# The first MLP matrices in token layout, with seven block products for eight on half of the rows

## The chip, the cores and the metric

One NeuronCore of a Trainium2 chip runs the whole program; the other seven are idle. The metric is the device time of one execution in microseconds (us), the median of several runs.

## The reference, cut to what matters

A two-layer decoder trunk on 256 positions of width 2048, all in float32: a recurrent mixer (layer 0) or dilated attention (layer 1), an output projection with residual, then an MLP with residual. The change is in the MLP:

```python
D_MODEL, SEQ, DEPTH = 2048, 256, 2
D_FF = 4 * D_MODEL
def squared_relu_mlp(h, w1, w2):
    return jnp.square(jax.nn.relu(h @ w1)) @ w2
...
h = h + squared_relu_mlp(rms_norm(h, norm_mlp[layer]), mlp_w1[layer], mlp_w2[layer])
```

The two MLPs hold 2 x 2 x 2048 x 8192 weights, about 62% of all weight bytes that the kernel reads.

## The kernel before, in words

**Precision.** Every large product is made from three: each operand x is split into hi (a rounded copy) and lo = x - hi, and hi*hi, hi*lo and lo*hi are added up in PSUM. `Weights.split` (L102 to L106) does this for weights: ScalarE (ACT) copies hi (L105), VectorE (DVE) subtracts to lo (L106).

**Units.** All weights come as units of 128 x 2048 floats, 1 MB each. `units` is the list of them in the order of use; `unit()` (L166) hands out the next one and calls `fetch()` (L111) so that the loads run about two units ahead. Loads go out on the queue of SyncE (SP). `hi`, `lo` and `raw` have three buffers each. `hi` of a unit can be written when TensorE (PE) has finished the unit three places before it.

**Each MLP runs in four quarters** of 2048 hidden features (`mlp`, L685). A quarter has two stages.

- *First matrix (w1).* 16 units, each for 128 hidden features. `project` (L354) with `cross` (L206) holds the weights still and streams the activations: for each of 16 blocks of the input one matmul of 512 columns (weight hi against activation hi and lo side by side) and one of 256 (weight lo against activation hi). The result has features on partitions, so `folded` (L225), the squared relu (L691) and `split_to` (L233) write it straight into `bufb`, the input of the second matrix. `sums` (L623) prepares four combinations of blocks in `forms`.
- *Second matrix (w2).* Here activations are held still and 512 weight columns stream (`products`, L633). On half of the rows the 2 x 2 block product is done with seven products instead of eight: the weight blocks a, t1, t2, c, t3, d, t4 of `PRODUCTS` (L883) are sums of units, made by `combine` (L127) in place: `a` += t1, `a` += t2, `a` += d on DVE (L143) and t1 += the unit of t2 by an accumulating DMA from the queue of GpSimd (POOL, L139). The units "n" are plain rows. One such unit is 12 matmuls, a plain one 24 (two halves j of the tokens). A quarter has two such pairs (n0 = 0 and n0 = 2) of 11 units. `to_x` (L654) adds the banks into the residual `xall`. The tiles `a` and `t1` have one buffer each, so the next pair's `a` can be loaded only when the last split that reads `a` is done.

**Order.** A list scheduler orders each engine's instructions at build time; on the chip ACT and DVE run theirs strictly in that order. Matmuls of the large products and the transposes through PE (`turn`, L179) are chained by hand in program order (`chain`, L174). Work in `later` is run by `flush()` (L184). `urgent` raises the priority of what empties PSUM, `stream` that of loads and splits.

**Transposes before.** `to_features` (L598) turns the residual back to features on partitions for the next stage, 8 transposes of 128 x 128 a time, only after the output projections and after the MLP of layer 0.

Of the kernel before, what the change touches and what calls it, by code (L numbers as in the profile page):

```python
# [20 lines left out]
P = 128  # L21
# [20 lines left out]
def trunk_kernel(ctx, tc, x, xtok, cols, tab, masks, pos, fin, w_in, w_gate, w_out, w_qkv, w_o, w1, w2, out):  # L42
# [28 lines left out]
    def plan2(i, products):  # L71
        if not products:
            units.extend((w2, i + u) for u in range(8))
            return
        for what, u in PRODUCTS:
            units.append((w2, None if u is None else i + u, what))
# [34 lines left out]
    def fetch():  # L111
        u = at[0]
        if u >= len(units):
            return
        at[0] += 1
        src, i = units[u][:2]
        with stream():
            if len(units[u]) > 2:
                combine(u, src, i, units[u][2])
# [3 lines left out]
            made[u] = Weights(r, 2048 if src is w2 or src is w1 and i % 64 > 2 else 1024)  # L123
# [3 lines left out]
    def combine(u, src, i, what):  # L127
# [10 lines left out]
        if T3_DMA and what == "t2":  # L138
            nc.gpsimd.dma_start(held["t1"], src[i], accum_op=OP.add)  # L139
        if T3_DMA and what == "t3":  # L140
            add = None
# [83 lines left out]
    def folded(p, name="z", bufs=None, home=None):  # L225
        with urgent():
            t = tmp.tile([P, S], F32, name="t1", bufs=2)
            A.copy(t, p[:, S:])  # L228
            z = (home or tmp).tile([P, S], F32, name=name, bufs=bufs)
            V.tensor_tensor(z, p[:, :S], t, OP.add)  # L230
        return z

    def split_to(dst, src, gain=None):  # L233
        if gain is None:
            A.copy(dst[:, :S], src)  # L235
            V.tensor_tensor(dst[:, S:], src, dst[:, :S].bitcast(F32), OP.subtract)
# [26 lines left out]
    class FirstNorm:  # L263
# [3 lines left out]
        def add(self, blk):  # L267
            self.n += 1
            q = tmp.tile([P, S], F32, name="t1", bufs=2)
            A.activation(q, blk, AF.Square)  # L270
            if self.n == 1:
                self.ss.append(tmp.tile([P, S], F32, name="q", bufs=1))
# [94 lines left out]

    nrm = FirstNorm()
# [47 lines left out]
    def scaled(p, z, acc=None):  # L416
        with urgent():
            if acc is direct:
                V.tensor_tensor(z, p[:, :S], rs, OP.mult)
            else:  # L420
                t = tmp.tile([P, S], F32, name="t1", bufs=2)
# [9 lines left out]
    vgs = mixers.enter_context(tc.tile_pool(name="vgs", bufs=1))  # L431
    wk = mixers.enter_context(tc.tile_pool(name="wk", bufs=2))
# [131 lines left out]
    def lru_out(b):  # L564
# [3 lines left out]
        q = tmp.tile([P, S], F32, name="q", bufs=1)  # L568
# [17 lines left out]
    rot = mixers.enter_context(tc.tile_pool(name="rot", bufs=1))  # L586
# [11 lines left out]
    def to_features(n, gname):  # L598
        def work():
            with urgent():  # L600
                for half in range(2):
                    p = psc.tile([P, 2, S], F32, name="pl", bufs=2)
                    for j in range(2):
                        for i in range(2):
                            k = 4 * n + 2 * half + i
                            turn(p[:, i, j * P:j * P + P], xres[:, j, k * P:k * P + P])
                    for i in range(2):
                        k = 4 * n + 2 * half + i
                        split_to(bufa[:, k], p[:, i], col(gname, k))
        later.append(work)  # L610

    def out_project(src, gname, kgs):
        nrm = Norm()
        for n in range(4):
            add_res(tokens(src, 4 * n, bufb, kgs), n, nrm)
            to_features(n, gname)
# [4 lines left out]
    spot = []  # L621

    def sums(k, z1, z2):  # L623
        t = pair.tile([P, 512], F32, name="sums")
        a11, a21, a12, a22 = z1[:, :P], z1[:, P:], z2[:, :P], z2[:, P:]
        V.tensor_tensor(t[:, :P], a21, a22, OP.subtract)
        V.tensor_tensor(t[:, P:2 * P], t[:, :P], a11, OP.subtract)
        V.tensor_tensor(t[:, 2 * P:3 * P], a11, a21, OP.subtract)
        V.tensor_tensor(t[:, 3 * P:], a12, t[:, P:2 * P], OP.add)
        A.copy(forms[:, k, 0], t)  # L630
        V.tensor_tensor(forms[:, k, 1], t, forms[:, k, 0].bitcast(F32), OP.subtract)

    def products(i0, n0, nrm, r2, r2n, done):  # L633
        n1 = n0 + 1
        i0 += 4 * n0
        plain = lambda j, k: (bufb[:, k, j * P:j * P + P], bufb[:, k, S + j * P:S + j * P + P])
        form = lambda f, k: (forms[:, k, 0, f * P:f * P + P], forms[:, k, 1, f * P:f * P + P])
        side = {"a": lambda i: plain(0, 2 * i), "d": lambda i: plain(0, 2 * i + 1), "t4": lambda i: plain(1, 2 * i + 1),
                "t1": lambda i: form(0, i), "t2": lambda i: form(1, i), "t3": lambda i: form(2, i),
                "c": lambda i: form(3, i)}  # L640
        alpha, delta, gamma = (pmm.tile([P, 512], F32, name="p") for _ in range(3))
        beta = psc.tile([P, 512], F32, name="po" if n0 else "pd", bufs=1)
        opened = []
# [10 lines left out]
        def to_x(bank, j, n, sign=1, last=False):  # L654
            at = slice(n * 512, n * 512 + 512)
            with urgent():
                V.scalar_tensor_tensor(xres[:, j, at], bank, (r2 if sign > 0 else r2n)[:, j:j + 1], xres[:, j, at],  # L657
                                       op0=OP.mult, op1=OP.add)
                if nrm and last:
                    nrm.add(j, n)  # L660

        after_product = {"a": [(beta, 0, n0, 1)], "t1": [(alpha, 1, n1, 1)], "t2": [(beta, 0, n1, -1)],
                         "t3": [(beta, 1, n1, -1, True)]}
        bank = {"a": beta, "t1": alpha, "t2": beta, "c": alpha, "t3": beta, "d": gamma, "t4": beta}
        for what, u in PRODUCTS:
            w = unit(w2, None if u is None else i0 + u)
            if what != "n":
                times(bank[what], w, side[what])
                for job in after_product.get(what, ()):
                    to_x(*job)  # L670
                if what == "t3":
                    done(n1)
                if what == "t4":
                    flush()
                continue
            n, g = divmod(u, 4)
            for j in (1, 0) if n else (0, 1):
                times({(0, 0): gamma, (0, 1): beta, (1, 0): alpha, (1, 1): delta}[n, j], w,
                      lambda i, j=j, g=g: plain(j, 4 * g + i))
                if g == 3:  # L680
                    to_x({(0, 0): gamma, (0, 1): beta, (1, 0): alpha, (1, 1): delta}[n, j], j, n + n0, 1, (n, j) != (1, 1))
            flush()
        done(n0)

    def mlp(layer, nrm, nxt, gname):  # L685
        r2 = None
        for q in range(4):
            for m in range(16):
                z = folded(project(w1, layer * 64 + q * 16 + m, bufa), "zp", 3, pair)
                with urgent():  # L690
                    V.scalar_tensor_tensor(z, z, 0.0, z, op0=OP.max, op1=OP.mult)  # L691
                    split_to(bufb[:, m], z)
                if m < 8 and m % 2:
                    sums(m // 2, zs, z)
                zs = z
                if r2 is None:
                    r2 = nrm.inv_mean()
                    r2n = tmp.tile([P, 2], F32, name="r2n", bufs=1)
                    V.tensor_scalar(r2n, r2, -1.0, None, op0=OP.mult)
                    if not gname:  # L700
                        lut(spare, epsc, AF.Sqrt)
                    spot[:] = [after(V.memset(spare, 0.0), [])]
            ends = nxt if q == 3 else None

            def done(n):
# [4 lines left out]
                elif n != LAST:  # L710
                    at = slice(n * 512, n * 512 + 512)
                    with urgent():
                        for j in range(2):
                            V.tensor_tensor(xres[:, j, at], xres[:, j, at], fing[:, at], OP.mult)

            for n in range(4):
                if n < 2 * PAIRS:
                    if n % 2 == 0:
                        products(layer * 64 + q * 16, n, ends, r2, r2n, done)
                else:  # L720
                    ps = tokens(w2, layer * 64 + q * 16 + 4 * n, bufb)
                    add_res(ps, n, ends, r2)
                    done(n)

    pairs = ExitStack()
    pair = pairs.enter_context(tc.tile_pool(name="pair0", bufs=1))
    forms = pair.tile([P, 4, 2, 512], F32R, name="forms", align_bytes=LINE)
# [4 lines left out]

    ppi = rot.tile([32, S], I32, name="ppi")
    nc.gpsimd.dma_start(ppi, bass.AP(tensor=pos.tensor, offset=pos.offset, ap=[[0, 32], [1, S]]))
    ang = rot.tile([32, S], F32, name="ang")
    cosT = rot.tile([32, S], F32, name="cosT")
    sinT = rot.tile([32, S], F32, name="sinT")
    after(V.tensor_copy(ang, ppi), spot)
    V.tensor_scalar(ang, ang, tab_[:32, TC_FREQ:TC_FREQ + 1], None, op0=OP.mult)
    MAGIC = 12582912.0  # L740
    V.tensor_scalar(cosT, ang, 1.0 / (2.0 * math.pi), None, op0=OP.mult)
    V.tensor_scalar(cosT, cosT, MAGIC, None, op0=OP.add)
    V.tensor_scalar(cosT, cosT, MAGIC, None, op0=OP.subtract)
    rest = 2.0 * math.pi
    for bits in (5, 13, 21, None):
        part = rest if bits is None else math.floor(rest * 2.0 ** bits) / 2.0 ** bits
        rest -= part
# [241 lines left out]
```

## Time and profile before

| | us |
|---|---|
| median of 3 runs | 2202.48 (2202.17 to 2202.95) |
| the profiled execution | 2203.3 |
| its span, first to last instruction | 2201.2 |
| DVE busy | 1673.1 (76%) |
| ACT busy | 1110.8 (50%) |
| weight loads of PE (PEld) busy | 1897.6 (86%) |

In rows of the profile the name left of the arrow is the tile that is written, those right of it are read; "x16" is a count; for grouped instructions "busy, mean ns" follow the bar, then the idle time of the engine before them and who ended it. A timeline row is start, length, engine, line, operation. A row of the chain of waits is start, length, what. PEclk is the share of full clock that PE was granted. 431.25 MB were moved by DMA, 196 GB/s in the mean.

### The profile page before, as it was taken

How to read it: one execution, taken by the hardware profiler on the slowest of the kernel's cores; microseconds unless marked ns; L12 is line 12 of the kernel's file. 1: busy time of each engine (PE TensorE's matmuls, PEld its weight loads, DVE VectorE, ACT ScalarE, POOL GpSimd, SP SyncE). 2: the span in 40 equal slices, each digit the busy share in tenths (PEclk: the TensorE clock that was granted, in tenths of full speed). 3: DMA queues.
4: the chain of work that ended last, by engine and by line, in shares of the span. 5: the costliest groups of instructions: out<-in, count | busy, mean ns of one | idle time of the engine just before them, and what ended most of it. 6: DMA issues, size and time to landing. Idle time of an engine off the chain costs nothing.

```text
span 2201.2 us, 29711 instructions
## 1 busy us (share of the span) xinstructions
PE 2180.7 (99%) x12004; PEld 1897.6 (86%) x12004; DVE 1673.1 (76%) x2294; ACT 1110.8 (50%) x1371; POOL 14.7 (1%) x21
## 2 busy tenths in 40 slices
PE   9999999999999999999999999999999999999998
PEld 8999998888888888888888888888888888888886
DVE  7766796578877877877867778556797687687787
ACT  7444485545444444544655445445454445445444
POOL 0000000000000000000000000000000000000000
PEclk9999999999999999999999999999999999999999
DMA  8444446555655755765655554655566567566553
GB/s 314 154 162 164 154 154 229 184 197 192 233 197 184 248 194 167 245 216 157 217 200 173 172 179 166 225 191 185 164 215 246 176 205 249 191 191 248 188 195 115
DMA packets 61081, 431.25 MB, mean 196 GB/s; under 512 B 6784, under 2 KB 7552, under 8 KB 9488
## 3 DMA queue, kind: packets, MB, share of 16 engines
q1 hardware_dynamic: 58320, 411.94, 53.4%
q0 software_dynamic: 2336, 16.81, 4.1%
q8 instruction: 94, 1.54, 0.3%
q10 hardware_dynamic: 288, 0.61, 0.1%
q14 instruction: 43, 0.35, 0.0%
HBM read 427.23 MB, written 2.10 MB: 195 GB/s over the span
## 4 chain that ended last, share of the span: by engine, by line
PE 85%; DVE 9%; ACT 3%; DMA 2%; issue 1%; SPq 0%; ACTq 0%
PE p L177 76%; DVE lo L106 5%; PE po L177 5%; DVE a L143 2%; ACT hi L105 2%; DMA a<-in_w 2%; PE pd L177 1%; PE pl L479 1%; DVE xall L657 1%; DMA raw<-in_w_in 0%; PE pl L180 0%; PE pl L784 0%; PE po L805 0%; PE pd L797 0%; PE pd L463 0%
## 5 line engine op out<-in xcount | busy, mean ns | idle before, releaser
L106 DVE TENSOR_TENSOR lo<-raw,hi 128x1024 fp32r<-128x1024 f32 (+2 forms) x492 | 822.7, 1690 | 340.9 <-ACT hi L105 322.9
L105 ACT CAST hi<-raw 128x1024 fp32r<-128x1024 f32 (+2 forms) x492 | 688.9, 1426 | 671.2 <-PE p L177 511.2
L177 PE MATMUL p<-bufa,hi 128*128 128x512 f32 (+1 forms) x3840 | 854.0, 356 | 0.1
L177 PEld LDWEIGHTS p<-bufa,hi 128*128 128x128 f32 x3840 | 670.9, 189 | 92.3 <-DVE bufa L239 0.6
L177 PE MATMUL p<-bufa,lo 128*128 128x256 f32 x3200 | 521.6, 284 | 0.0
L177 PEld LDWEIGHTS p<-bufa,lo 128*128 128x128 f32 x3200 | 452.2, 191 | 12.8
L177 PE MATMUL p<-hi,bufb 128*128 128x512 f32 x1408 | 451.6, 391 | 1.6 <-DVE xall L657 1.6
L177 PEld LDWEIGHTS p<-hi,bufb 128*128 128x128 f32 x1408 | 264.3, 188 | 59.6 <-DVE xall L657 5.0
L177 PE MATMUL p<-lo,bufb 128*128 128x512 f32 x704 | 275.0, 391 | 3.9 <-DVE lo L106 3.9
L105 ACT CAST hi<-a 128x2048 fp32r<-128x2048 f32 x64 | 122.4, 1913 | 161.9 <-PE p L177 81.1
L106 DVE TENSOR_TENSOR lo<-a,hi 128x2048 fp32r<-128x2048 f32 x64 | 146.6, 2290 | 58.4 <-ACT hi L105 58.3
L177 PEld LDWEIGHTS p<-lo,bufb 128*128 128x128 f32 x704 | 132.2, 188 | 33.8 <-DVE lo L106 7.3
L177 PE MATMUL p<-hi,bufa 128*128 128x512 f32 x384 | 124.7, 399 | 1.4 <-ACT hi L105 1.4
L177 PEld LDWEIGHTS p<-hi,bufa 128*128 128x128 f32 x384 | 72.9, 190 | 16.8 <-ACT hi L105 1.8
L177 PE MATMUL pd<-hi,bufb 128*128 128x512 f32 x256 | 84.2, 390 | 0.2 <-DVE xall L657 0.2
L177 PE MATMUL po<-hi,bufb 128*128 128x512 f32 x256 | 84.1, 389 | 0.3 <-DVE xall L657 0.3
L177 PE MATMUL p<-hi,forms 128*128 128x512 f32 x256 | 84.0, 389 | 0.0
L177 PE MATMUL p<-lo,bufa 128*128 128x512 f32 x192 | 76.6, 399 | 0.9 <-DVE lo L106 0.9
L143 DVE TENSOR_TENSOR a<-a,raw 128x2048 f32<-128x2048 f32 x32 | 73.1, 2285 | 0.0
L228 ACT COPY t<-p 128x256 f32<-128x256 f32 x128 | 46.9, 367 | 41.2 <-PE p L177 40.7
L657 DVE SCALAR_TENSOR_TENSOR xall<-p,nm,xall 128x512 f32<-128x512 f32 x64 | 47.8, 747 | 18.9 <-PE p L177 18.9
L235 ACT CAST bufb<-zp 128x256 fp32r<-128x256 f32 x128 | 50.3, 399 | 18.7 <-DVE zp L691 18.7
(241 smaller groups left out, 1803.9 us busy)
## 6 DMA issues: line engine op xcount, KB each, us to landing
raw<-in_w SPq DMA_DIRECT2D x224, 1024.0 KB, 4.8
raw<-in_w_qkv SPq DMA_DIRECT2D x48, 1024.0 KB, 4.8
raw<-in_w_in SPq DMA_DIRECT2D x46, 1024.0 KB, 4.8
raw<-in_w_out SPq DMA_DIRECT2D x16, 1024.0 KB, 4.8
a<-in_w SPq DMA_DIRECT2D x16, 1024.0 KB, 4.8
t<-in_w SPq DMA_DIRECT2D x16, 1024.0 KB, 4.9
t<-in_w POOLq DMA_DIRECT2D x16, 1024.0 KB, 7.8
raw<-in_w_o SPq DMA_DIRECT2D x16, 1024.0 KB, 4.8
```

The lines of the kernel that those rows point to most:

```text
L105: A.copy(h, w)
L106: V.tensor_tensor(l, w, h.bitcast(F32), OP.subtract)
L143: V.tensor_tensor(r, r, held[add], OP.add)
L177: chain[:] = [after(T.matmul(*args, **kw), chain)]
L228: A.copy(t, p[:, S:])
L235: A.copy(dst[:, :S], src)
L479: T.matmul(pl[:, j], kq[:, js], halves(qp[:, js], c, True), start=True, stop=True)
L657: V.scalar_tensor_tensor(xres[:, j, at], bank, (r2 if sign > 0 else r2n)[:, j:j + 1], xres[:, j, at], op0=OP.mult, op1=OP.add)
```

## The change

- **w1 in token layout.** The weights of w1 are laid out as w2's are. `blocks` is the old `products` made general: `first` uses it for w1 and `second` for w2. A w1 quarter is now two pairs of 11 units, with activations held still, and its results are 128 tokens x 512 features.
- **Results turned on PE.** `final`, `hold` and `u3` take the banks out of PSUM: ACT copies (`hold`), DVE adds or subtracts, ACT Relu and ACT Square. `to_h` then turns each 128 x 512 tile with four transposes, splits the result into `bufb` and, for the first 8 blocks of the quarter, makes the combinations (`combos`, `part_forms`) for w2 in `formh`. It is queued in `later` and run by the `flush()` behind a plain unit.
- **The inputs of w1 need combinations too.** `to_features` makes them in `formx` behind the output projections.
- **Sums by DMA.** t1 += t2's unit by DMA as before, now for w1 too; for w1 also `a` += d's unit (`T4_DMA`), for w2 that sum stays on DVE.
- **Order of units.** w1: a t1 n6 t2 c n7 t3 d n2 t4 n3. w2: a t1 n7 t2 c n6 t3 d n2 t4 n3. Before: a t1 n6 t2 c n7 t3 d t4 n2 n3.
- **Small moves.** The rotary angles are made behind the first v group of layer 1, not before; the final gain is loaded in four pieces into free tiles of the MLP on POOL's queue; small pools move; the scratch memory for software DMA is set to 4096 bytes.

The diff, cut to its core:

```diff
+    def plan2(src, i):
+        for what, u in ORDERS[src is w2]:
+            units.append((src, None if u is None else i + u, what, i))
...
-            units.extend((w1, layer * 64 + q * 16 + i) for i in range(16))
-            for n in range(0, 4, 2):
-                plan2(layer * 64 + q * 16 + 4 * n, n < 2 * PAIRS)
+            for src in (w1, w2):
+                for n in range(0, 4, 2):
+                    plan2(src, layer * 64 + q * 16 + 4 * n)
...
+        if what == "t2":
             nc.gpsimd.dma_start(held["t1"], src[i], accum_op=OP.add)
+        if what == "c" and src in T4_DMA(w1, w2):
+            nc.gpsimd.dma_start(held["a"], src[i0 + 1], accum_op=OP.add)
...
+        plains = [0, 0]
+        for what, u in ORDERS[src is w2]:
+            w = unit(src, None if u is None else i0 + 4 * n0 + u)
+            if what != "n":
+                times(bank[what], w, side[what])
+                if what in events:
+                    events[what](bank[what])
+                continue
+            n, g = divmod(u, 4)
+            plains[n] += 1
+            for j in (1, 0) if n else (0, 1):
+                times(sums[n, j], w, lambda i, j=j, g=g: plain(j, 4 * g + i))
+                if plains[n] == 2:
+                    final(n, j, sums[n, j])
+            flush()
+
+    def to_h(n, tiles):
+        def work():
+            ps = []
+            for y in tiles:
+                ps.append(psc.tile([P, 4, P], F32, name="pl", bufs=2))
+                for i in range(4):
+                    turn(ps[-1][:, i], y[:, i * P:i * P + P])
+            with urgent():
+                for j, p in enumerate(ps):
+                    h = bufb[:, 4 * n:4 * n + 4, j * P:j * P + P]
+                    A.copy(h, p)
+                    V.tensor_tensor(bufb[:, 4 * n:4 * n + 4, S + j * P:S + j * P + P], p, h.bitcast(F32), OP.subtract)
+                if n < 2:
...
+                    combos(a22, s2, a21, s4, a11, a21, a12, a22)
+                    for v, at in ((z, slice(1, 4, 2)), (t, slice(0, 4, 2))):
+                        part_forms(formh, 2 * n, 2, at, v.rearrange("p (m two) c -> p m two c", two=2))
+        later.append(work)
+
+    def first(i0, n0):
...
+        def relu2(n, j, y, src):
+            A.activation(y, src, AF.Relu)
+            A.activation(y, y, AF.Square)
+            tiles[n, j] = y
+            if (n, 1 - j) in tiles:
+                to_h(n0 + n, (tiles[n, 0], tiles[n, 1]))
+
+        def u3(bank):
+            with urgent():
+                y = keep["y4"]
+                V.tensor_tensor(y, y, bank, OP.subtract)
+                V.tensor_tensor(y, keep["delta"], y, OP.add)
+                relu2(1, 1, y, y)
+
+        def final(n, j, bank):
+            with urgent():
+                if (n, j) == (1, 1):
+                    keep["delta"] = bank
+                elif (n, j) == (0, 1):
+                    y = pair.tile([P, 512], F32, name="y21")
+                    relu2(0, 1, y, bank)
+                else:
+                    y = keep["y2" if n else "y1"]
+                    V.tensor_tensor(y, bank, y, OP.subtract if n else OP.add)
+                    relu2(n, j, y, y)
+
+        blocks(w1, i0, n0, bufa, formx, {"a": hold("y1", 2), "t1": hold("y4"), "t2": hold("y2"), "t3": u3}, final)
...
-PRODUCTS = (("a", 0), ("t1", 4), ("n", 6), ("t2", 5), ("c", None), ("n", 7), ("t3", None), ("d", 1),
-            ("t4", None), ("n", 2), ("n", 3))
+SCRATCH = 4096
+_A = (("a", 0), ("t1", 4))
+_B = (("t2", 5), ("c", None))
+_C = (("t3", None), ("d", 1), ("n", 2), ("t4", None), ("n", 3))
+ORDERS = (_A + (("n", 6),) + _B + (("n", 7),) + _C, _A + (("n", 7),) + _B + (("n", 6),) + _C)
+T4_DMA = lambda w1, w2: (w1,)
```

More of the change, by code (lines that the diff above doesn't have):

```diff
@@ L585, in trunk_kernel, with open_pairs, part_forms, combos @@
     mixers.close()
-    rot = mixers.enter_context(tc.tile_pool(name="rot", bufs=1))
+    pairs = ExitStack()
+    def open_pairs(layer):
+        pool_ = pairs.enter_context(tc.tile_pool(name=f"pair{layer}", bufs=1))
+        return pool_, [pool_.tile([P, 4, 2, 512], F32R, name=n) for n in ("formx", "formh")]
+    def part_forms(f, k, m, at, src):
+        hi, lo = (f[:, k:k + m, h].rearrange("p m (f c) -> p m f c", f=4)[:, :, at] for h in range(2))
+        A.copy(hi, src)
+        V.tensor_tensor(lo, src, hi.bitcast(F32), OP.subtract)
+    def combos(s1, s2, s3, s4, a11, a21, a12, a22):
+        V.tensor_tensor(s1, a21, a22, OP.subtract)
+        V.tensor_tensor(s3, a11, a21, OP.subtract)
+        V.tensor_tensor(s2, s1, a11, OP.subtract)
+        V.tensor_tensor(s4, a12, s2, OP.add)
+    pair, (formx, formh) = open_pairs(0)
     def add_res(ps, n, nrm, scale=None):
@@ L606, in work @@
                             turn(p[:, i, j * P:j * P + P], xres[:, j, k * P:k * P + P])
-                    for i in range(2):
-                        k = 4 * n + 2 * half + i
-                        split_to(bufa[:, k], p[:, i], col(gname, k))
+                    k = 4 * n + 2 * half
+                    if forms is None:
+                        for i in range(2):
+                            split_to(bufa[:, k + i], p[:, i], col(gname, k + i))
+                        continue
+                    z = pair.tile([P, 2, 2, P], F32, name="y21")
+                    for i in range(2):
+                        A.activation(z[:, i], p[:, i].rearrange("p (j c) -> p j c", j=2), AF.Copy,
+                                     scale=col(gname, k + i))
+                    zs = z.rearrange("p i j c -> p i (j c)")
+                    split_to(bufa[:, k:k + 2], zs)
+                    a11, a21, a12, a22 = (z[:, i, j] for i in range(2) for j in range(2))
+                    combos(a22, a11, a21, a12, a11, a21, a12, a22)
+                    part_forms(forms, k // 2, 1, slice(0, 4), z.rearrange("p i j (one c) -> p one (i j) c", one=1))
         later.append(work)
@@ new lines, in first, with hold, event @@
+    def first(i0, n0):
+        keep, tiles = {}, {}
+        def hold(name, bufs=1):
+            def event(bank):
+                with urgent():
+                    keep[name] = pair.tile([P, 512], F32, name=name, bufs=bufs)
+                    A.copy(keep[name], bank)
+            return event
+        def relu2(n, j, y, src):
[11 more added lines that the diff above has]
+        def final(n, j, bank):
+            with urgent():
+                if (n, j) == (1, 1):
[8 more added lines that the diff above has]
+        blocks(w1, i0, n0, bufa, formx, {"a": hold("y1", 2), "t1": hold("y4"), "t2": hold("y2"), "t3": u3}, final)
@@ L655, in to_x, with second @@
+    def second(i0, n0, nrm, r2, r2n, done, gains):
+        def to_x(bank, j, n, r, last):
             at = slice(n * 512, n * 512 + 512)
             with urgent():
-                V.scalar_tensor_tensor(xres[:, j, at], bank, (r2 if sign > 0 else r2n)[:, j:j + 1], xres[:, j, at],
-                                       op0=OP.mult, op1=OP.add)
+                V.scalar_tensor_tensor(xres[:, j, at], bank, r[:, j:j + 1], xres[:, j, at], op0=OP.mult, op1=OP.add)
                 if nrm and last:
@@ L660, in to_x, with u2 @@
                     nrm.add(j, n)
[L662 to L682, printed above, removed]
+        def u2(bank):
+            to_x(bank, 0, n0 + 1, r2n, False)
+            if gains:
+                gains()
@@ L683, in products, with u3 @@
+        def u3(bank):
+            to_x(bank, 1, n0 + 1, r2n, True)
+            done(n0 + 1)
+        blocks(w2, i0, n0, bufb, formh,
+               {"a": lambda b: to_x(b, 0, n0, r2, False), "t1": lambda b: to_x(b, 1, n0 + 1, r2, False),
+                "t2": u2, "t3": u3},
+               lambda n, j, b: to_x(b, j, n0 + n, r2, (n, j) != (1, 1)))
         done(n0)
     def mlp(layer, nrm, nxt, gname):
-        r2 = None
-        for q in range(4):
[L688 to L702, printed above, removed]
@@ new lines, in mlp, with gains @@
+        fing = []
+        def gains():
+            for n, name in enumerate(("y1", "y1", "y2", "y4")):
+                fing.append(pair.tile([P, 512], F32, name=name, bufs=2 if n < 2 else 1))
+                nc.gpsimd.dma_start(fing[n], bass.AP(tensor=fin.tensor, offset=fin.offset + 512 * n,
+                                                     ap=[[0, P], [1, 512]]))
+        r2 = nrm.inv_mean()
+        r2n = tmp.tile([P, 2], F32, name="r2n", bufs=2)
+        V.tensor_scalar(r2n, r2, -1.0, None, op0=OP.mult)
@@ L703, in mlp @@
+        if not gname:
+            lut(spare, epsc, AF.Sqrt)
+        for q in range(4):
             ends = nxt if q == 3 else None
@@ L713, in done @@
                         for j in range(2):
[L714 to L727, printed above, removed]
+                            V.tensor_tensor(xres[:, j, at], xres[:, j, at], fing[n], OP.mult)
+            for n in (0, 2):
+                first(layer * 64 + q * 16, n)
+            for n in (0, 2):
+                second(layer * 64 + q * 16, n, ends, r2, r2n, done, gains if ends and not gname and not n else None)
+        return fing
     nx1 = Norm()
@@ L812, in trunk_kernel @@
             vg = tokens_group(w_qkv, g * 12, rt, kgs=(0, 1, 2, 3) if g else (0, 1, 3, 2))
+        if not g:
+            rotary()
         for hd in range(4 * g, 4 * g + 4):
@@ L824, in trunk_kernel @@
     mixers.close()
+    pair, (formx, formh) = open_pairs(1)
     nrm = out_project(w_o, "nmlp1", (0, 1, 2, 3))
-    late = ctx.enter_context(tc.tile_pool(name="late", bufs=1))
-    fing = late.tile([P, D], F32, name="fing")
-    nc.sync.dma_start(fing, bass.AP(tensor=fin.tensor, offset=fin.offset, ap=[[0, P], [1, D]]))
-    pair = pairs.enter_context(tc.tile_pool(name="pair1", bufs=1))
-    forms = pair.tile([P, 4, 2, 512], F32R, name="forms", align_bytes=LINE)
     fnorm = Norm()
-    mlp(1, nrm, fnorm, None)
-    pairs.close()
+    fing = mlp(1, nrm, fnorm, None)
     done = [n for n in range(4) if n != LAST]
```

141 lines of the change are left out of this document (63 added, 78 removed).

## The prediction

> **What bounds the kernel now.** I read the page first: busy shares, then the chain of waits, then the stages by windows.
>
> ```profile
> PE 2180.7 (99%) x12004; PEld 1897.6 (86%) x12004; DVE 1673.1 (76%) x2294; ACT 1110.8 (50%) x1371; POOL 14.7 (1%) x21
> PE 85%; DVE 9%; ACT 3%; DMA 2%; issue 1%; SPq 0%; ACTq 0%
> 360.00:427.00 67.00, 67.00 (x310) 55.73 (x309) 36.61 (x42) 31.87 (x48) 0.00 (x0) 1.00 0.55 184
> 517.00:598.00 81.00, 80.31 (x353) 65.86 (x352) 70.00 (x44) 40.89 (x23) 0.88 (x1) 1.00 0.70 237
> 1111.00:1135.00 24.00, 24.00 (x113) 19.90 (x112) 15.71 (x30) 12.12 (x19) 0.00 (x0) 1.00 0.57 202
> ```
>
> The window rows give length, then busy time of PE, PEld, DVE, ACT and POOL, the granted clock, DMA share and GB/s. PE sets the time. Only the w2 stage (517 to 598) is tight elsewhere: DVE is busy 70 of 81 us there, and the chain leaves PE for DVE and ACT. So fewer matmul columns pay, as long as PE waits for nobody.
>
> Two starts of PE's timeline bracket the stages of one quarter: w2 begins at 516.73, the next w1 at 599.64, the next w2 at 688.68. The third and fourth row, from the chain, price one block product and one set of 8 transposes.
>
> ```profile
> 516.73 0.40 PE L177 MATMUL pd<-hi,bufb 128*128 128x512 f32 x1
> 599.64 0.62 PE L177 MATMUL p<-bufa,hi 128*128 128x512 f32 x2
> 688.68 0.40 PE L177 MATMUL pd<-hi,bufb 128*128 128x512 f32 x1
> 528.26 2.72 PE pd L177 x12
> 409.66 0.87 PE pl L180 x8
> ```
>
> **Columns.** A w1 stage takes 688.68 - 599.64 = 89.04 us. The new one has two pairs of 7 x 12 + 4 x 24 = 180 matmuls at 2.72 / 12 = 0.2267 us: 2 x 40.8 = 81.6 us. Over 8 quarters: **-59.4 us**.
>
> **Transposes.** Each quarter turns 8 tiles of 128 x 512, four sets of 8 transposes at 0.87 us; 32 sets: **+27.8 us**. Without any wait the change would so give -31.6 us, or 1.97 us for each of the 16 calls of `first`.
>
> **Waits for the turned tiles.** In the built program PE's order is: plain unit n3 (j = 0, then j = 1), transposes of y1, transposes of y21, then unit a of the next pair. y21 is the Relu and Square of the bank that the matmul just ahead has finished. PE must stand still at least for that; with ACT idle it would be
>
> ```profile
> 511.16 3.82 PE L177 MATMUL p<-bufa,hi 128*128 128x512 f32 x16
> 511.42 0.37 ACT L228 COPY t<-p 128x256 f32<-128x256 f32 x1 [5.06 <-PE p L177]
> L294 ACT ACTIVATE z<-xall 128x512 bf16<-128x512 f32 x32 | 20.1, 627 | 30.7 <-DVE xall L593 16.7 <-DVE xall L657 12.4 <-DVE fr L854 1.6
> L105 ACT CAST hi<-a 128x2048 fp32r<-128x2048 f32 x64 | 122.4, 1913 | 161.9 <-PE p L177 81.1 <-DVE a L143 50.3 <-PE pd L177 18.5
> L106 DVE TENSOR_TENSOR lo<-a,hi 128x2048 fp32r<-128x2048 f32 x64 | 146.6, 2290 | 58.4 <-ACT hi L105 58.3
> L143 DVE TENSOR_TENSOR a<-a,t 128x2048 f32<-128x2048 f32 x16 | 36.6, 2287 | 0.2
> L593 DVE SCALAR_TENSOR_TENSOR xall<-p,xall 128x512 f32<-128x512 f32 x16 | 11.0, 688 | 10.9 <-PE p L177 10.9
> a<-in_w SPq DMA_DIRECT2D x16, 1024.0 KB, 4.8
> t<-in_w POOLq DMA_DIRECT2D x16, 1024.0 KB, 7.8
> ```
>
> 0.26 from PE's end to ACT (511.16 to 511.42) and two ACT passes of 0.63: 1.5 us, 24 us in 16 calls. That is the lower bound. But ACT runs its list in order, and the built list around each of the 16 seams is, for n0 = 0 (n0 = 2 lacks the three lines marked *; "=" is my gloss):
>
> ```
> bufb<-pl  bufb<-pl          = hi of the turned y2, y4
> hi<-a                       = next pair's a
> y4<-pl *
> hi<-a                       = next pair's t1, after DVE's a += t1
> Relu y21<-pd                = needs n3's last matmul
> hi<-raw                     = the unit after t1
> Relu y1
> formh<-y4 *  formh<-y2 *
> Square y21
> Square y1                   = the first set of transposes waits for this
> ```
>
> I lay this out from the end of plain unit n2 (zero), with the rows above. PE: transposes of y2, y4 to 0.87, t4 to 3.6, n3 to 9.03. DVE: n2's hi can be cast when the unit three before it ends, at -10.9; it is ready at -8.7, its lo at -6.4, two passes on y4 to -5.0, lo of t4 at -2.75. Only then may `a` be loaded: landed at 2.05. Cast to 4.05, lo to 6.35, a += t1 to 8.6, (n0 = 0: one pass of 0.4 ahead of it, so 9.0), hi of t1 to 10.5 (10.9), Relu y21 to 11.1 (11.5), hi of the next unit to 13.0 (13.4), Relu y1 to 13.7 (14.1), two casts of 0.62 (to 15.3), Squares to 14.9 (16.5). PE has stood since 9.03: 5.9 us (7.5 us). Neighbours in a queue overlap a little, so I take 5.8 and 7.4: 8 x 13.2 = **+106 us**. Behind the waiting transposes the whole of PE is queued; DVE runs ahead meanwhile, and the first units after the seam find their splits ready. The other sets (y2, y4) are ready about 2 us before n2 ends and wait for nothing.
>
> **Seams without transposes.** After a w2 pair nothing gives DVE time to catch up, and t4 now has one plain unit behind it instead of two: 8.16 us of matmuls for load, cast, lo, a += t1, cast, lo. Before, the same chain read:
>
> ```profile
> 543.44 4.80 DMA a<-in_w
> 548.34 1.92 ACT hi L105
> 550.29 2.30 DVE lo L106
> 552.61 2.30 DVE a L143
> 555.01 1.92 ACT hi L105
> 558.01 0.39 PE L177 MATMUL po<-hi,bufb 128*128 128x512 f32 x1
> 560.74 0.39 PE L177 MATMUL p<-hi,forms 128*128 128x512 f32 x1
> ```
>
> The load went out 14.6 us ahead of the pair's first matmul (558.01), and t1's lo, 2.3 us behind its hi (556.93), was ready at 559.2, 1.5 us ahead of its use at 560.74. Now the load goes out at -3.4 on the same clock (no y4 passes but one `to_x`), 11.6 us ahead: 3 us later, and one `to_x` more sits ahead of a += t1. t1 so starts 1.9 us late; DVE, back to back from there, makes t2 and n6 late by 1 us each: 4.1 us between the two w2 pairs, and 2.3 us from w2 into the next w1, whose DVE list is shorter. The old w2 stage had 599.64 - 516.73 - 81.6 = 1.3 us of this. Sum: 8 x (4.1 - 1.3) + 6 x 2.3 = **+36 us**. Bounds: -10 (all such waits gone) to +60.
>
> **The clock.** Waits of 6 us are new in this kernel. Its start shows what short ones do:
>
> ```profile
> 12.26 0.39 PE L177 MATMUL p<-hi,bufa 128*128 128x512 f32 x1
> 14.06 0.49 PE L177 MATMUL p<-hi,bufa 128*128 128x512 f32 x1 [1.42 <-ACT hi L105]
> 15.32 0.50 PE L177 MATMUL p<-lo,bufa 128*128 128x512 f32 x1 [0.77 <-DVE lo L106]
> 17.18 0.63 PE L177 MATMUL p<-lo,bufa 128*128 128x512 f32 x1
> 18.46 0.63 PE L177 MATMUL p<-lo,bufa 128*128 128x512 f32 x1
> 6.00:16.40 10.40, 8.06 (x33) 5.42 (x33) 8.60 (x30) 8.09 (x19) 0.00 (x0) 1.00 1.01 378
> 16.40:19.80 3.40, 3.40 (x10) 2.63 (x9) 3.40 (x11) 3.30 (x8) 0.00 (x0) 0.50 1.03 418
> 2194.10:2201.20 7.10, 0.00 (x0) 0.00 (x0) 1.48 (x5) 1.57 (x3) 0.00 (x0) 0.50 0.74 295
> ```
>
> Waits of 1.42 and 0.77 us were followed by 3.4 us at half clock, in which three matmuls took 18.46 - 17.18 = 1.28 us, 0.427 each: 3.4 x (1 - 0.227 / 0.427) = 1.6 us lost. At the end the clock is at half too. I count one such loss for each of the 16 long waits: **+26 us**; bounds 0 and 52 (two stretches each). The Trainium skill (TensorE: Matmul & The Clock Gate, Part 1) gives the rule that speaks against this change: a free-running window of about 3.4 us without work halves PE's clock, and a window with work restores it. Its window fits the half-clock row of 3.4 us; as an estimate by that page, a wait of 7.4 us always holds a whole window and one of 5.8 us in (5.8 - 3.4) / 3.4 = 70% of cases, so 13.6 losses instead of 16, 22 us instead of 26 and a sum of 2335.
>
> **Edits at nothing.** The inputs' combinations behind the output projections are some 8 small passes on DVE and ACT for each half tile, beside PE in a stage where DVE is busy 36.6 of 67 us; the rotary angles lie beside the v group (15.7 of 24 us); without that cover they would cost 10 and 6 us. The software DMA of `a` += d goes out when t2's lo is done; t2, c, n7 and t3 (13.6 us of matmuls) lie ahead of the cast that needs it, against 7.8 us to land. The gain's four pieces have most of a quarter.
>
> **Sum.** 2203.3 - 59.4 + 27.8 + 106 + 36 + 26 = 2339.7 for the profiled execution; the median before is 0.8 lower, so **2339 us**.
>
> **Rivals.**
>
> - *Waits only* (20%): the clock stays full and the late t1 is absorbed, since DVE got ahead during the long waits. For it: a long wait comes twice a quarter. Against it: between the w2 pairs there is none. 2203.3 - 31.6 + 106 = 2278 us.
> - *The clock falls twice as long*, and also at the w2 seams (14%): 26 us more for the long waits and some 16 x 0.8 for the others, about 2378 us. For it: waits of 2.2 us in all sufficed at the start.
> - *The columns decide* (7%), the other side: PE waits at each of the 16 seams only for Relu and Square, 1.5 us, under the 1.97 us at which the change breaks even, and the w2 seams stay as they are. 2203.3 - 31.6 + 24 = 2196 us, 0.3% faster. For it: PE is 99% busy and ACT half idle. Against it: ACT's list puts 1.9 us casts and DVE's a += t1 between the last matmul and the Square.
> - *The sums by DMA are late* (5%), so that the change does not take DVE's work away for free: with two software DMAs a pair and a small scratch memory the cast of t4 waits. From 13 us to land on, each further us costs 16 us; at 16 us to land it is 2339 + 48 = 2387 us. Against it: 7.8 us now.
>
> **How the numbers follow.** The forecast has 50%; 4% are left for what I do not see. The range 2265 to 2385 takes in the forecast, the first two rivals and the spread of the wait terms (106 could be 85 to 120), about 84%. Faster by over 0.2% (4.4 us, about what a measurement of this kernel can tell from no change): 0.07. Within 0.2%: 0.02, the waits being just at break-even. Slower: 0.91.
>
> **What the new profile would show.** PE idle of some 100 us put down to ACT's Square of y1, in 16 places of 5 to 8 us; 32 sets of transposes at 0.87; w1 stages of about 102 us and w2 stages of about 86; a granted clock at half for about 3.4 us behind most long waits; the chain with an ACT share several times the 3% of now. Waits under 2 us would make the prediction wrong at its root; a w2 stage of 83 us the seam term; a clock at 1.00 throughout the clock term.

## The result, and the profile after

The changed kernel takes 2363.02 us (median of 4 runs, 2359.30 to 2368.76) against 2202.72 us (2202.17 to 2203.19) for the kernel before: a ratio of 1.073, 95% interval 1.0708 to 1.0752. The profiled execution took 2363.19 us with a span of 2361.0 us. It is 159.9 us longer than the profiled execution before; 2339 was predicted for it, in a range of 2265 to 2385.

From the page of the kernel after: busy time of the engines, the chain of waits by engine, and the group of the transposes of y tiles (busy and mean ns, then the idle time of PE just ahead of them, and its releaser).

```profile
PE 2201.3 (93%) x11044; PEld 1864.1 (79%) x11044; DVE 1788.7 (76%) x2078; ACT 1265.5 (54%) x1429; POOL 44.6 (2%) x57
PE 59%; DVE 16%; ACT 11%; DMA 7%; issue 6%; ACTq 0%; SPq 0%; DVEq 0%
L179 PE MATMUL pl<-tab__181,y 128*128 128x128 f32 x256 | 48.1, 350 | 106.4 <-ACT y L715 106.4
```

PE's idle time is its span less its busy time: 2361.0 - 2201.3 = 159.7 us, and 2201.2 - 2180.7 = 20.5 us before. So 139.2 of the 159.9 us are idle time, and 20.6 us are busy time, although PE has 960 instructions fewer. ACT's share of the chain went from 3% to 11%. The waits of PE name the causes (total, times, longest):

```profile
PE pl L179 <- ACT y L715: 106.4, 16, 9.4
PE p L176 <- DVE lo L103: 31.4, 24, 2.4
PE p L176 <- ACT hi L102: 3.6, 6, 1.0
PE p L176 <- DVE bufa L231: 2.7, 2, 1.4
PE po L176 <- DVE lo L103: 1.8, 4, 0.5
PE pd L176 <- DVE lo L103: 1.6, 6, 0.3
```

The first row is the turned tiles: 16 waits for the Square (L715), of 5.1 to 9.4 us each. The rows on L102 and L103 are waits for the halves of the weights, 38.4 us together. L231 makes lo of the inputs of w1; the kernel before has no such wait. One seam, that is, the step from one pair to the next, the first with n0 = 0, in PE's and ACT's timeline (start, length, instruction, idle time before it):

```profile
461.69 1.04 PE L179 MATMUL pl<-tab__181,y 128*128 128x128 f32 x8
462.48 0.47 PE L176 MATMUL pd<-hi,bufa 128*128 128x512 f32 x1
470.52 0.39 PE L176 MATMUL pd<-hi,bufa 128*128 128x512 f32 x1
477.96 1.97 PE L179 MATMUL pl<-tab__181,y 128*128 128x128 f32 x8 [7.05 <-ACT y L715]
479.58 0.77 PE L176 MATMUL po<-hi,bufa 128*128 128x512 f32 x1
```
```profile
471.11 1.90 ACT L102 CAST hi<-a 128x2048 fp32r<-128x2048 f32 x1 [4.47 <-DVE a L142]
472.92 0.59 ACT L714 ACTIVATE y<-pd 128x512 f32<-128x512 f32 x1
473.41 1.89 ACT L102 CAST hi<-raw 128x2048 fp32r<-128x2048 f32 x1
475.20 0.63 ACT L714 ACTIVATE y<-y 128x512 f32<-128x512 f32 x1
475.73 1.12 ACT L588 CAST formh<-y 128x512 fp32r<-128x512 f32 x2
476.76 1.15 ACT L715 ACTIVATE y<-y 128x512 f32<-128x512 f32 x2
```

Read it from 461.69, where unit n2 has ended. PE's last matmul of n3 is done near 470.9. ACT stood idle for 4.47 us until DVE had added t1 to a, cast that sum, and only then, at 472.92, 11.2 us after n2, came to the Relu of the bank that PE had finished 2 us before; behind it stood a cast of 1.89 us for another unit, and the Squares ended 16.2 us after n2. The layout in the prediction had 10.9 and 16.5 us at these two points. For n0 = 2 the same row reads 5.28 us (5.8 predicted):

```profile
528.83 1.97 PE L179 MATMUL pl<-tab__181,y 128*128 128x128 f32 x8 [5.28 <-ACT y L715]
```

The stages by windows of the kernel after (length, busy PE, PEld, DVE, ACT, POOL, then the granted clock): a w1 stage, the w2 stage behind it, and the time around the first long wait cut in three.

```profile
426.50:530.40 103.90, 90.21 (x401) 74.34 (x400) 78.95 (x64) 63.96 (x64) 3.46 (x4) 0.94 0.69 210
530.40:618.50 88.10, 84.80 (x363) 69.14 (x362) 68.26 (x43) 38.81 (x22) 0.87 (x1) 0.97 0.59 203
471.00:473.60 2.60, 0.00 (x0) 0.00 (x0) 2.26 (x6) 2.49 (x3) 0.86 (x1) 0.99 0.49 50
473.60:483.80 10.20, 5.84 (x18) 4.97 (x19) 9.51 (x10) 6.07 (x9) 0.00 (x0) 0.50 0.71 193
483.80:490.00 6.20, 6.20 (x28) 5.12 (x28) 3.70 (x5) 5.41 (x6) 0.40 (x1) 1.00 0.00 0
```

The clock fell to half 2.7 us after PE went idle and stayed there for 10.2 us, in 5.84 of which PE worked. At each of the 16 long waits the trace has such a stretch, begun while PE waits: two of 3.4 us, ten of 6.8 us and four of 10.2 us, with 73.4 us of PE's work in them. Four more of 3.4 us stand behind short waits, one of them at the start of the kernel; with them it is 86.1 us of work at half clock. The transposes behind the wait, at half clock, took 479.58 - 477.96 = 1.62 us a set, against 462.48 - 461.69 = 0.79 us for the set at full clock.

### The profile page after: what moved, and what is told of

The parts are those of the page before. It is cut to its first block, busy times and chain, and to the rows that moved or that the text cites. A ratio compares the mean times of both kernels' runs of the same rounds, so it can differ in the third digit from the quotient of the medians.

```text
span 2361.0 us, 27739 instructions
## 1 busy us (share of the span) xinstructions
PE 2201.3 (93%) x11044; PEld 1864.1 (79%) x11044; DVE 1788.7 (76%) x2078; ACT 1265.5 (54%) x1429; POOL 44.6 (2%) x57
## 3 DMA queue, kind: packets, MB, share of 16 engines
q0 software_dynamic: 7264, 51.42, 11.6%
## 4 chain that ended last, share of the span: by engine, by line
PE 59%; DVE 16%; ACT 11%; DMA 7%; issue 6%; ACTq 0%; SPq 0%; DVEq 0%
PE p L176 47%; DVE lo L103 9%; ACT hi L102 9%; DMA a<-in_w 6%; DVE a L142 4%; PE pd L176 4%; PE po L176 4%; PE pl L179 2%; DMA raw<-in_w 1%; PE pl L471 1%; ACT y L714 1%; ACT y L715 1%; DVE xall L745 1%; DVE y L723 0%; DMA xall<-in_x 0%
## 5 line engine op out<-in xcount | busy, mean ns | idle before, releaser
L103 DVE TENSOR_TENSOR lo<-raw,hi 128x1024 fp32r<-128x1024 f32 (+2 forms) x454 | 748.4, 1667 | 195.5 <-ACT hi L102 178.5
L102 ACT CAST hi<-raw 128x1024 fp32r<-128x1024 f32 (+2 forms) x454 | 626.9, 1408 | 441.9 <-PE p L176 379.0
L103 DVE TENSOR_TENSOR lo<-a,hi 128x2048 fp32r<-128x2048 f32 x128 | 293.0, 2289 | 181.8 <-ACT hi L102 181.8
L102 ACT CAST hi<-a 128x2048 fp32r<-128x2048 f32 x128 | 244.3, 1908 | 328.8 <-DVE a L142 199.2
L176 PE MATMUL p<-hi,bufa 128*128 128x512 f32 x1280 | 411.0, 392 | 3.5 <-DVE bufa L231 2.7
L176 PE MATMUL p<-bufa,hi 128*128 128x256 f32 (+1 forms) x1792 | 364.9, 317 | 0.1
L176 PEld LDWEIGHTS p<-bufa,hi 128*128 128x128 f32 x1792 | 294.5, 190 | 18.9 <-DVE hz L413 0.3
L176 PEld LDWEIGHTS p<-hi,bufa 128*128 128x128 f32 x1280 | 241.0, 188 | 54.8 <-DVE bufa L231 3.6
L176 PE MATMUL p<-bufa,lo 128*128 128x256 f32 x1152 | 255.5, 287 | 0.0
L176 PE MATMUL p<-lo,bufa 128*128 128x512 f32 x640 | 251.1, 392 | 1.0 <-DVE lo L103 1.0
L176 PEld LDWEIGHTS p<-bufa,lo 128*128 128x128 f32 x1152 | 189.3, 191 | 2.7
L179 PE MATMUL pl<-tab__181,y 128*128 128x128 f32 x256 | 48.1, 350 | 106.4 <-ACT y L715 106.4
L176 PEld LDWEIGHTS p<-lo,bufa 128*128 128x128 f32 x640 | 120.6, 188 | 27.0 <-DVE lo L103 2.6
```

What stands on the lines that cost most here:

```text
L102: A.copy(h, w)
L103: V.tensor_tensor(l, w, h.bitcast(F32), OP.subtract)
L176: chain[:] = [after(T.matmul(*args, **kw), chain)]
L179: chain[:] = [after(T.transpose(out_, in_, ident), chain)]
```

## The experiments

The theory: PE waits for turned tiles because the Square stands at the end of ACT's list (106 us); the clock falls behind these waits; and a is loaded late because t4 has one plain unit behind it instead of two. The rival: PE would wait anyway, for weights or for the sums by DMA, and the turned tiles only stand where the wait happens to fall. The first, second and fourth to sixth experiment are single runs; but for the sixth, the effects are many times the spread above (9.5 us).

**Turns later** (e1_late_turn). Turns that are due when a plain unit begins are made behind it; those that it makes due wait for the next one.

```
             plains[n] += 1
+            due = later[:]
+            later.clear()
             for j in (1, 0) if n else (0, 1):
...
-            flush()
+            for f in due:
+                f()
```

> The kernel after, but the last two tiles of a pair (y1, y21) are turned behind the next pair's first plain unit, 8.2 us of matmuls later, instead of right behind the matmul that ends them; the order of the units stays. Theory (106 us of waits because the turns stand behind ACT's list, about 39 us of half clock behind them, and some 46 us because the next pair's a is loaded late): the waits put down to ACT's Square fall from 106 us to under 10, the half clock behind them goes too, but a and t1 of the next pair now come late at these 16 seams as they do behind w2, 1.5 to 3 us each: 2363 - 106 - 39 + 24 to 48 = 2242 to 2266 us. Rival (PE would starve for the next pair's weights anyway, and the turns only stand where the wait falls): the waits move to the lo of a and t1 with the same 5 to 8 us each, about 2350 us.

It took 2315.64 us, 47 us less, far above what the theory allowed. The waits of PE in this run, and the window behind one of them:

```profile
PE p L176 <- DVE lo L103: 60.4, 42, 2.6
PE p L176 <- ACT y L713: 22.8, 8, 3.2
PE p L176 <- ACT hi L102: 8.2, 9, 1.8
483.90:487.30 3.40, 3.40 (x10) 2.65 (x9) 1.71 (x1) 0.00 (x0) 0.66 (x1) 0.51 0.59 87
```

The waits for turned tiles are gone, all 106 us, and two others have grown: those for lo from 31.4 to 60.4 us, and a new one of up to 3.2 us on L713, ACT's copy of t1's product out of its PSUM bank, which n6 needs again. That copy stands in ACT's list behind two casts for later units, the first of which waits for the next sum in a. The last row is 3.4 us at half clock behind such a wait, all of it with PE at work. The trace has 18 stretches at half clock, and PE's busy time hardly fell (2200.5 us). The long wait had been cover for the late a; the theory had priced that cover too low, and the rival is half right here.

**The old order of the units** (e2_old_order), with the turns as in the kernel after:

```
-_C = (("t3", None), ("d", 1), ("n", 2), ("t4", None), ("n", 3))
+_C = (("t3", None), ("d", 1), ("t4", None), ("n", 2), ("n", 3))
```

> The kernel after with the order of the units of before (t4 ahead of the two last plain units, so that a is free and loaded one plain unit, 5.4 us, earlier), turns where they are. Theory: the seams without turns lose their waits, w2 stages 83 to 84 us instead of 88 and first matmuls of the next w1 without 2 to 3 us of waits, -36 to -46 us; ACT's list before the Square has the casts of a and t1 earlier, so the long waits fall too, to about 3.4 us each (0.26, Relu, one cast of 1.9, Square), 55 us instead of 106, with less half clock: 2203 - 32 + 55 + 26 + about 5 = 2255 to 2265 us. Rival (the late load is not what the seams wait for; DVE simply has too much to do): w2 stages stay at 88 us, and the time falls by under 50 us.

It took 2286.17 us, 77 us less and 21 us above the theory. Its waits, and a w2 stage:

```profile
PE pl L179 <- DVE y L595: 50.8, 8, 6.4
PE pl L179 <- ACT y L715: 28.4, 12, 3.1
PE p L176 <- DVE lo L103: 10.4, 18, 1.1
```
```profile
709.60:792.10 82.50, 82.02 (x364) 67.58 (x362) 69.53 (x44) 40.70 (x22) 1.73 (x2) 1.00 0.65 218
```

The seams are as expected: w2 stages of 82.5 and 84.4 us, waits for lo down to 10.4 us. The Square is earlier too. But in the first pair of each quarter (8 of 16) the turns now wait for something else, L595, the last combination that DVE makes of y2 and y4. It reads their turned form in the PSUM bank into which y1 is to be turned, and in DVE's list it stands behind two or three passes of 2.3 us on weights. The wait of 6.4 us is again an engine's list, only another engine's.

**Both** (e3_late_turn_old_order).

> Both edits: turns of y1 and y21 behind the next pair's first plain unit, and t4 ahead of the two last plain units. Theory: neither waits for turned tiles nor late a; what is left are the columns (-59.4) and the transposes (+27.8): 2203 - 32 = 2172 us, with small waits 2172 to 2195 us, faster than both kernels. Rival (DVE, with 8 more passes a quarter on the turned tiles, sets the pace of the w1 stages as well): PE idle 20 us and more spread over waits for lo, 2195 to 2230 us.

It took 2196.42 us (median of 10 runs, 2195.06 to 2200.93), 0.9975 of the time before (0.9965 to 0.9984): a quarter of a per cent faster than the kernel before. That is 1.4 us above the theory's range and just inside the rival's, but the rival's mark, 20 us and more of waits for lo, is not there. The page's first line, the waits, and the w1 stage of its second quarter:

```profile
PE 2156.3 (98%) x11044; PEld 1832.6 (84%) x11044; DVE 1783.8 (81%) x2078; ACT 1265.6 (58%) x1429; POOL 44.6 (2%) x57
PE p L176 <- DVE lo L103: 12.9, 18, 1.8
PE p L176 <- ACT y L713: 7.6, 8, 1.0
598.30:685.00 86.70, 85.19 (x385) 69.82 (x384) 73.64 (x54) 58.73 (x54) 3.46 (x4) 1.00 0.80 244
```

PE idles 2194.3 - 2156.3 = 38.0 us, the clock is whole (0.999), and PE's busy time is 24.4 us less than before: this run shows what columns and transposes are worth by themselves. Alone the two edits gave 47 and 77 us, together 167: each alone left or uncovered a wait that the other takes away.

**Only the clock** (e4_dummy_matmuls). PE works at nothing while it waits.

```
+            if src is w1 and u == 3:
+                idle = psc.tile([P, 512], F32, name="pt", bufs=1)
+                for m in range(20 if n0 else 28):
+                    mm(idle, w.part(0, P)[0], w.part(m % 4 * 512, 512)[0], start=True, stop=True)
             flush()
```

> The kernel after with matmuls that nobody reads (28 of 512 columns in the first pair of a quarter, 6.3 us at full clock, 20 in the second, 4.5 us) between the last plain unit's matmuls and the turns, where PE waits. Theory of the clock (about 39 us are lost at half clock behind the waits): the granted clock of the w1 stages comes back to 0.99 or more, the 8 transposes behind the waits take 0.87 us instead of 1.62, and the time falls by 25 to 39 us, to 2324 to 2338 us. Rival (the half clock lies in time in which PE would have had to wait for the next splits anyway): the clock is restored and the time stays within 10 us of 2363.

It took 2310.76 us, 52.4 us less and 13 us below the theory's range, at a mean clock of 0.997 instead of 0.971.

```profile
PE 2251.6 (98%) x11428; PEld 1904.2 (82%) x11428; DVE 1786.8 (77%) x2078; ACT 1263.9 (55%) x1429; POOL 44.7 (2%) x57
PE pl L179 <- ACT y L719: 1.7, 2, 1.4
```

Not all of it is the clock, since the edit also moved ACT's list: at the first seam the 1.9 us cast between the two Relus now comes behind the Squares. The 384 added matmuls are 384 x 0.2267 = 87.1 us. Without them PE was busy 2164.5 us, 36.8 less than in the kernel after: the clock. Idle time (2308.6 - 2251.6 = 57.0 us) and added matmuls together are 144.1 us against 159.7; the 15.6 us between them I put down to ACT's list; the rows show that at the first seam only. The rival, half clock only where PE would wait anyway, falls.

**The order in w2 alone** (e5_old_order_w2_only).

```
-ORDERS = (... _A + (("n", 7),) + _B + (("n", 6),) + _C)
+_D = (("t3", None), ("d", 1), ("t4", None), ("n", 2), ("n", 3))
+ORDERS = (... _A + (("n", 7),) + _B + (("n", 6),) + _D)
```

> The kernel after with the order of the units of before in the w2 pairs alone (t4 ahead of the two last plain units there); w1 pairs and turns as in the kernel after. It measures the seam term by itself. Theory (behind a w2 pair the next a is loaded 5.4 us too late, which costs about 5 us in each w2 stage and 2 to 3 us at the start of each next w1, 8 x 5 + 6 x 2.4 = 54 us with the half clock that these waits set off): w2 stages 83 to 84 us, the waits for turned tiles stay at about 106 us, 2308 to 2323 us. Rival (the seams are slow because the long waits in w1 have put the splits out of step): w2 stages stay at 87 to 89 us and the time at 2355 to 2365 us.

It took 2305.59 us, 57.6 us less, just below the theory's range.

```profile
PE pl L179 <- ACT y L715: 95.0, 16, 7.0
PE p L176 <- DVE lo L103: 10.6, 17, 0.9
528.40:612.60 84.20, 83.56 (x362) 68.75 (x361) 70.07 (x44) 40.86 (x23) 1.73 (x2) 0.98 0.63 214
714.20:797.70 83.50, 83.00 (x363) 68.24 (x362) 69.76 (x44) 40.83 (x23) 1.73 (x2) 0.99 0.64 215
```

The load of the next a and the first matmul of its pair, between the first two w2 pairs of the kernel after and then of this run:

```profile
560.18 0.33 SPq L127 DMA_DIRECT2D a<-in_w  x1
571.90 0.39 PE L176 MATMUL po<-hi,bufb 128*128 128x512 f32 x1
```
```profile
556.33 0.33 SPq L127 DMA_DIRECT2D a<-in_w  x1
570.91 0.39 PE L176 MATMUL po<-hi,bufb 128*128 128x512 f32 x1
```

The load goes out 11.7 us ahead in the kernel after (the prediction had 11.6) and 14.6 us ahead here, as in the kernel before. The w2 stages lose 3.9 and 5.4 us with the long waits of w1 in place, so those do not make the seams slow; the late a does. The waits for weights fell from 38.4 to about 12 us, the long waits by 11 us, and PE's busy time (2182.2 us) by 19.1 us, with less half clock.

**The sum for t4 by DVE** (e6_t4_by_dve). `T4_DMA` gives `()`, so DVE adds d to a in w1 too.

> The kernel after without the new software DMA: DVE adds d to a for t4 in the w1 pairs, as it does in w2 (16 passes more of 2.28 us). Theory (DVE and ACT are late at the seams, the sums by DMA are not): lo of t4, the load of the next a, and all that ACT's list has behind it come up to 2.3 us later at 16 seams, so the waits for turned tiles grow from 106 to 115 to 143 us: 2372 to 2405 us. Rival (the two software DMAs of a pair are late or crowd the loads): the waits shrink, 2330 to 2360 us.

It took 2361.59 us: neither. The 1.4 us less lie within the spread of the kernel after. DVE works 35 us more, and waits only change places:

```profile
PE pl L179 <- ACT y L715: 96.6, 16, 7.9
PE p L176 <- DVE lo L103: 37.4, 31, 2.4
```

10 us less here, 6 us more there, the total as it was. The new software DMA, which lands in 8.5 us (median) in the kernel after, is neither late nor a help. The 10 us are all at the eight seams with n0 = 0 (62.1 us of waits, here 52.2 us): the load of the next a landed there in 4.7 to 5.2 us instead of 4.9 to 6.8. No packet of a software DMA moved in the 6 us behind the issue of these loads in the kernel after; why they are quicker here stays open.

**Two attempts to better the version with both edits.** With the sum for t4 by DMA in w2 too (v1_both_and_t4_by_dma):

> Late turns and old order together (2196 us), and the sum for t4 by DMA in the w2 pairs too, which takes 16 passes of 2.28 us off DVE. Theory (the 13 us that PE still waits for lo are DVE's): some 4 to 10 us less, 2186 to 2192 us. Rival (the second software DMA of a pair lands too late for t4, or the waits for lo come from ACT and the loads): 2194 to 2205 us.

2198.18 us (2194.91 to 2200.48; 0.9976 of before, 0.9966 to 0.9986): nothing gained, though DVE is busy 34 us less (1750.0 us). With L713's copy of y4 made by DVE (v2_both_y4_by_dve):

```
-                    A.copy(keep[name], bank)
+                    V.tensor_copy(keep[name], bank) if name == "y4" else A.copy(keep[name], bank)
```

> Late turns and old order together (2196 us), with the copy of t1's product (y4) out of its PSUM bank made by DVE instead of ACT, where it stands behind the cast of the next pair's t2 (8 waits, 7.6 us in all). Theory (each such wait is one of ACT's list, and DVE's copy comes right behind the lo that PE needs next): the 7.6 us go, 2188 to 2192 us. Rival (DVE's list is no shorter: the copy holds up the lo of t2 by its 0.7 us, or waits itself): 2194 to 2203 us, with more waits for lo.

2233.00 us (2230.24 to 2236.82), 1.0138 of before (1.0121 to 1.0155), a clear miss:

```profile
PE p L176 <- DVE y L713: 29.9, 8, 3.8
```
```profile
479.17 2.28 DVE L103 TENSOR_TENSOR lo<-raw,hi 128x2048 fp32r<-128x2048 f32 x1
481.37 0.68 DVE L589 TENSOR_TENSOR formh<-y,formh 128x512 fp32r<-128x512 f32 x1
481.98 0.68 DVE L713 COPY y<-p 128x512 f32<-128x512 f32 x1
```

A copy of 0.68 us, put behind a pass of 2.28 us on weights and one of 0.68 us in the other list, made eight waits of 3.7 us out of eight of 1 us. PE's busy time rose by 15.0 us with them (2171.3 us): the clock again.

## Why the prediction was right, and which sizes were off

The sign, the mechanism and the place were right. PE's busy and idle time of the kernels before, after and "both" split the 159.9 us by the prediction's terms; 16 of the 32 sets of transposes ran at half clock, and their loss is under the clock.

| term | predicted | measured | from |
|---|---|---|---|
| columns | -59.4 | -49.7 | "both": 2156.3 - 2180.7 - 25.3 |
| transposes | +27.8 | +25.3 | 32 sets of 0.79 |
| turned tiles | +106 | +106.4 | the row on L715 |
| seams (other idle time) | +36 | +32.8 | 139.2 - 106.4 |
| clock (other busy time) | +26 | +45.0 | 2201.3 - 2156.3 |

- **Waits for turned tiles**: sound in mechanism and at the seam shown. The prediction took the order of the built list on ACT and DVE and laid durations on it; Relu and Square alone (1.5 us) would have given a quarter of it. That the total agrees to 0.4 us is partly luck: the eight waits with n0 = 0 are 7.8 us each (7.4 predicted), the eight with n0 = 2 are 5.5 us (5.8). With n0 = 0 the load of a took 4.9 to 6.8 us, not 4.8; the longest load stands ahead of the longest wait, 9.4 us.
- **Seams without transposes**: sound. The w2-order experiment shows the cause (t4's place, and with it the load of a): some 27 us of waits for weights go with it. The forecast of 86 us for a w2 stage was short by 2 to 3, which is half clock; the bound of -10 was never near. Two of its steps are off: from its own figures t1 starts 3 + 0.7 (one `to_x`) - 1.5 = 2.2 us late, not 1.9 (0.98 + 1.82 = 2.8 us at the first such seam, shown below), and of the 1.3 us that it took off for the old w2 stage 0.7 us were idle time. The row on L231 (2.7 us) is in the 32.8 us too.
- **The clock** is the term that was too small: one stretch of 3.4 us was counted for each long wait, 1.6 us lost. Only 2 of the 16 were that short; the work in them was 73.4 / 16 = 4.6 us, not 3.4, and short waits set off three stretches more in the MLPs. The 86.1 us of work at half clock give a loss of 40 us by the prediction's ratio (0.427 against 0.227 us a matmul) and of 44 us by that of the transposes (1.62 against 0.79 us). 36.8 us are shown by the dummy matmuls; that experiment kept two stretches of 3.4 us and 8.2 us of busy time more than "both", of which these stretches explain some 3 us. The rival "twice as long" had 26 + 26 + 13 = 65 us in this place: the measured 45 lie midway between it and the forecast.
- **Columns**: too large by 9.7 us. The price of 0.2267 us came from one product in the chain of waits. The kernel before had a better row, its two stages by windows:

```profile
599.64:688.68 89.04, 89.04 (x513) 78.71 (x512) 63.39 (x84) 43.18 (x51) 0.86 (x1) 1.00 0.56 185
516.73:599.64 82.91, 82.22 (x362) 67.42 (x361) 71.57 (x45) 41.11 (x24) 0.88 (x1) 1.00 0.69 233
```

  A w2 stage of 360 such matmuls kept PE busy for 82.22 us, 0.2284 each, and the w1 stage of "both" 85.19 - 3 x 0.79 = 82.8 us, 0.2300 each. Eight stages at 82.8 instead of 81.6 us make 9.6 of the 9.7 us.
- **Edits at nothing**: the sum by DMA made no difference beyond the spread in either direction; the rival in which it is late falls. The inputs of w1 were not quite free: once in each MLP PE waits 1.4 us for L231, which stands behind a pass of 2.3 us on weights in DVE's list, and every changed kernel has these two waits. What the combinations have in that, and the other edits at nothing, no run separates.
- **"The columns decide"** (2196 us) has the time of the version with both edits, 2196.42 us, but that is luck. The rival adds up -59.4 + 27.8 + 24; the run has -49.7 + 25.3 and 38.0 - 20.5 = 17.5 us more idle time, none of it behind a Square. Its condition, 1.5 us at each seam, the change as made does not meet.

## What to carry to other kernels

When a step is moved in front of PE's next work, find where its last pass stands in the built list of ACT or DVE, and lay the durations out from there: here a pass of 0.6 us cost 5 to 9 us because casts for later weights stood ahead of it. A consumer that is put one unit later costs PE no work and hides this, but only if nothing else was hiding behind the old wait: alone it gave 47 us here, with the late a mended as well 167. Count the clock for every wait that returns, short ones too, and price matmuls by a whole stage, not by one product.

## What the runs showed of the hardware

The half clock comes and goes in whole stretches of about 3.4 us: 10.2 us at the first seam above, 6.8 us at ten others, 3.4 us in other places, and not only behind long waits. Between two w2 pairs of the kernel after PE had waited 0.98 and 1.82 us:

```profile
575.76 0.51 PE L176 MATMUL p<-hi,formh 128*128 128x512 f32 x1 [0.98 <-ACT hi L102]
578.09 0.51 PE L176 MATMUL p<-lo,formh 128*128 128x512 f32 x1 [1.82 <-DVE lo L103]
575.70:579.40 3.70, 1.82 (x7) 1.28 (x8) 3.66 (x3) 1.81 (x2) 0.00 (x0) 1.00 1.05 186
579.40:582.80 3.40, 3.40 (x10) 2.63 (x9) 3.40 (x2) 0.00 (x0) 0.00 (x0) 0.50 0.75 142
```

PE was busy for half of the 3.7 us ahead, 1.82 us, and got half clock for the next 3.4 us. The Trainium skill (TensorE: Matmul & The Clock Gate, Part 1) has a free-running window of 3413 ns and a fall behind an idle one. The length agrees with these rows. That the window must be idle does not: 1.82 us idle in one piece was enough here, while a wait of 1.71 us at 621.6 in the same run was followed by no half clock.

Transposes of 128 x 128 in f32 run at the granted clock like other matmuls: 8 in 0.79 us at full clock, in 1.62 us at half.
